# Inputs laid out before the launch: x and memory with features on partitions, weights as one stream of chunks, bias by query and key

## The chip, the cores and the metric

The kernel runs on one core of a Trainium2 chip. A time is the device time of one execution in microseconds (us). What the launching function `kernel()` does with the arrays on the host before the launch is not part of it.

The engines are called as the profile calls them: PE (TensorE, matmuls and transposes), DVE (VectorE), ACT (ScalarE), POOL (GpSimd) and SP (SyncE, which issues most DMAs).

## The reference

One layer of a hybrid decoder trunk, cut to what matters. `x` is 256 tokens of 1024 features, `mem` 256 tokens of 1024; everything is float32.

```
h    = rms_norm(x, mix_norm_g)
qa, ka, va, qb, kb, vb = split(h @ w_in)          # 3072 columns
oa   = rms_norm(attention(qa, ka, va, bias), moba_out_g)   # 8 heads of 64, causal
ob   = rms_norm(diff_attention(qb, kb, vb, bias, lam), subln_g) * (1 - 0.2)  # 4 heads, two softmaxes each
x   += concat(oa, ob) @ w_out
m    = rms_norm(mem, mem_norm_g)
x   += softmax(q(rms_norm(x, cross_norm_g)) k(m)^T / 16) v(m) @ w_co         # w_cq, w_ck, w_cv; 4 heads of 256
h3   = rms_norm(x, ffn_norm_g)
x   += (silu(h3 @ w_gate) * (h3 @ w_up)) @ w_down          # width 2816
out  = rms_norm(x, final_norm_g)
bias[h, t, s] = rel_bias_table[bucket(t - s), h] for s <= t, else -1e30
```

With 256 tokens there is one block of the block-sparse attention, so its selection falls away. `rms_norm(x, g)` is `x * rsqrt(mean(x^2) + 1e-6) * g`.

## The kernel before

All weights pass through one loop of chunks of 1 MB each (128 partitions x 2048 numbers), 65 of them, in the order of their use. SP issues the DMA of a chunk into a raw buffer `wr` (three of them). Then each chunk is split into two float32r halves, a high part `wh` and a low part `wl`, in four quarters (`wpart`, L118): ACT copies `wr` to `wh` (L131), DVE subtracts `wh` from `wr` into `wl` (L116). The activations are split in the same way, and a product is the sum of three matmuls: high by high, high by low, low by high (`ws`, L319, line L325 of the profile). One step of `ws` does this for 128 features and two column halves: six matmuls of 256 columns. A chunk is eight steps.

The order of all work is written by hand. Each engine works its own list in order. `run` (L170) emits a chunk's steps one after the other; after each step `tick` (L148) raises a counter, the slot, and emits whatever was registered for that slot with `at(slot, ...)` or `later(n, ...)`. `tick` also emits quarters of `wpart`, about one for every two slots; `wuse` (L160) emits the quarters of the chunk about to be used that are still missing. So an entry `at(61, mem_t, 0)` puts the first transposes of the memory behind the 61st step on PE, and their evacuations at that place in the lists of ACT and DVE.

The start (L670 to L712). Six matmuls on zeros (`NWARM`) run while the first DMAs are on their way. `x` arrives with tokens on partitions; PE transposes it in 16 pieces (`x_t`, L359) into PSUM, ACT and DVE multiply by the gain and bring it to SBUF (`x_gain`, L367), and `x_split` makes the high and low part. The first chunk of `w_in` is not split: `wf` (L383) multiplies it in plain float32, two matmuls for each of eight feature blocks k, so that PE can start before a split exists. `x_keep` (L379) copies the transposed `x` from PSUM to `xT` for the residual. `x_stats` sums the squares of `x` on ACT; POOL takes the power -1/2; `x_row` (slot 13) spreads it over the partitions with two transposes on PE and a copy `RX` on ACT. `RX` scales the outputs of the projections.

After the first chunk: its product becomes qa0, evacuated by `qk_evac` (DVE), then split by `q_high` (four ACT instructions `qs`, L431) and `q_low` (two DVE, L437), one slot after the other. The second chunk gives ka0 (`qk_evac`, `k_high` on ACT L443, `k_low` on DVE L448), the third qa1, the fourth ka1, then V, then the same for qb and kb.

The bias: a strip of 384 distances for each head is built on POOL from the transposed table (`strips`, L229), written to DRAM and read back with overlapping rows by 12 DMAs (`bias_load`, L258). The gains arrive as rows and are transposed on PE (`load_g`).

The memory: it arrives with tokens on partitions. `mem_stats` (slots 52 and 54) sums squares on ACT, `mem_scale` (58 and 59) scales it on DVE, and `mem_t` (61, 64, 67 and 70) transposes four feature blocks each on PE and splits them on ACT (L310) and DVE (L312). Logits of the second head group follow from slot 73 on (`logits`, matmuls L483 and L484, DVE L489). From `mix_t` on the two kernels have the same list on every engine.

Of the kernel before, what the change touches and what calls it, by code (L numbers as in the profile page):

```python
# [17 lines left out]
P = 128  # L18
# [6 lines left out]
NWARM = 6  # L25
# [10 lines left out]

@with_exitstack
def layer(ctx: ExitStack, tc: tile.TileContext, x, mem, mix_norm_g, w_in, moba_out_g, diff_lambda,
          diff_subln_g, w_out, rel_bias_table, cross_norm_g, mem_norm_g, w_cq, w_ck, w_cv, w_co,
          ffn_norm_g, w_gate, w_up, w_down, final_norm_g, out):  # L40
# [30 lines left out]
    chunks = []  # L71

    def cols(w, c):
        return w[0, :, c * 256:(c + 1) * 256].rearrange("(k p) c -> p k c", p=P), (KT, 256)

    def rows(w, r, c, nk, nc_):
        return (w[0, r * P:(r + nk) * P, c * nc_:(c + 1) * nc_].rearrange("(k p) c -> p k c", p=P),
                (nk, nc_))

    for base in (0, 6):  # L80
        qk = [cols(w_in, base + i) for i in range(4)]
        chunks += [qk[0], qk[2], qk[1], qk[3]]
# [108 lines left out]
    raws[0] = w0  # L191
    state["dma"] = 1
    wdma(2)
    wdma(2)
    memn = slot(3, FT)
# [18 lines left out]

    strip = mx.tile([96, 384], FT, name="strip")
    bias = {}
    nc.gpsimd.memset(strip, NEG)
    tT = const.tile([96, 32], FT, name="tT")
    gvB = const.tile([29, P], FT, name="gvB")
    lp = const.tile([P, 4, 64], FT, name="lp")  # L220
    QL = slot(6).rearrange("p a b -> p (a b)").rearrange("p (n c h s) -> p n c h s", n=2, c=2, h=2)
    nr = 32
    strip_d = dram.tile([nr, 12, 384], FT, name="strip_d")
    sd = strip_d[:, :, :]
# [23 lines left out]
    def small_loads():  # L248
        r = 0
        for gv in (cross_norm_g, mem_norm_g, ffn_norm_g, moba_out_g, diff_subln_g):  # L250
            n = gv.shape[1] // P
            nc.gpsimd.dma_start(gvB[r:r + n, :], gv[0].rearrange("(k p) -> k p", p=P))
            r += n
        nc.gpsimd.dma_start(lp.rearrange("p a b -> p (a b)"),
                            bass.AP(tensor=diff_lambda.tensor, offset=diff_lambda.offset,
                                    ap=[[0, P], [1, 256]]))

    def bias_load(h0, n):  # L258
        t = mx.tile([P, n, 256], FT, name="bias", tag="bias", bufs=2)
# [39 lines left out]

    def transposed(src, j, bank):  # L300

        for a in range(2):
            for t in range(2):
                nc.tensor.transpose(bank[:, a, t * P:(t + 1) * P],
                                    src[:, t, (2 * j + a) * P:(2 * j + a + 1) * P], ident)
# [48 lines left out]
    xT = const.tile([P, KT, S], FT, name="xT")  # L354
    h = hH, hL = hl(both(12))
    hF = slot(4, FT)
    xb = []

    def x_t(k):  # L359

        if k % 4 < 2:
            xb.append(att("xb") if k < 5 else obank("xb").rearrange("p (a b) -> p a b", a=2))
        for t in range(2):
            nc.tensor.transpose(xb[k // 4 * 2 + k % 2][:, k % 4 // 2, t * P:(t + 1) * P],
                                xv[:, t, k * P:(k + 1) * P], ident)

    def x_gain(k):  # L367

        b = xb[k // 4 * 2 + k % 2][:, k % 4 // 2, :]
        if k % 2:  # L370
            nc.vector.tensor_scalar(hF[:, k, :], b, g(G_MIX + k), None, op0=OP.mult)
        else:
            nc.scalar.activation(hF[:, k, :], b, AF.Copy, scale=g(G_MIX + k))
# [5 lines left out]
    def x_keep(j):  # L379
        k = j // 2 * 4 + j % 2  # L380
        nc.vector.tensor_copy(xT[:, k:k + 3:2, :], xb[j])
# [7 lines left out]
    RX = {}  # L389

    def x_stats():
        ss = const.tile([P, 2], FT, name="ssx")
        for t in range(2):
            nc.scalar.activation(sq, xv[:, t, :], AF.Square, accum_out=ss[:, t:t + 1])
        RX[1] = rstd(ss, 2, D, "rx")

# [6 lines left out]
    def load_lambda():  # L403
        ls = const.tile([P, 4], FT, name="ls")
# [9 lines left out]
    KS = slot(0).rearrange("p a b -> p (a b)").rearrange("p (n c h s) -> p n c h s", n=2, c=2, h=2)  # L414
# [199 lines left out]

    def mem_scale(t):
        nc.vector.tensor_scalar(memv[:, t, :], memv[:, t, :], M["r"][:, t:t + 1], None, op0=OP.mult)

    m = (slot(4), slot(5))

    def mem_t(j):  # L620
        bank = att()
        transposed(memv, j, bank)
        split_g(*m, j, bank, G_MEM)
# [14 lines left out]
    for t in range(2):  # L638
        at(52 + 2 * t, mem_stats, t)
    at(56, mem_rstd)  # L640
    for t in range(2):
        at(58 + t, mem_scale, t)
# [9 lines left out]
    for j in range(4):  # L652
        at((61, 64, 67, 70)[j], mem_t, j)
# [16 lines left out]
    load_g(gvA, 0, 8)  # L670
# [10 lines left out]
    for k in (0, 1):  # L681
        x_t(k)
        x_gain(k)
# [9 lines left out]
    for j in range(2):  # L693
        x_keep(j)
# [360 lines left out]
```

## Time and profile before

| | |
|---|---|
| median of 3 runs | 426.32 us (426.26 to 426.61) |
| profiled execution | 426.91 us, of which its span (first to last instruction) is 425.1 us |
| PE busy | 414.4 us, 97% of the span, 2699 matmuls |
| DVE, ACT, POOL busy | 292.7, 253.5 and 27.5 us (69, 60 and 6%) |
| mean granted clock of PE | 0.996 |
| DMA | 74.59 MB, mean 175 GB/s |

The profile is of one execution. Its span leaves 1.8 us of its time outside. "Busy" adds up instructions, and matmuls overlap one another, so a busy PE is not one at its peak; what matters for the end is where PE stands still and how much it has in its list. A releaser ("<-DVE wl L116") is the instruction that ended an idle time, by the profile.

### The profile page before, as it was taken

The numbers are of one execution on the slowest core, as the hardware profiler recorded it, in microseconds if no ns is written. First come the engines' busy times: TensorE is split into PE (matmuls) and PEld (weight loads), VectorE is DVE, ScalarE is ACT, GpSimd is POOL, SyncE is SP. The second block draws the span as 40 slices with busy tenths as digits, with TensorE's granted clock in tenths as the row PEclk, the third lists the DMA queues.
The fourth block names the chain that finished last, engine by engine and source line by source line (L and its number), as shares of the span: only waits on it lengthen the run. The fifth ranks groups of instructions, "written<-read, shape, count | busy, mean of one in ns | idle before, by whom it ended". The sixth has DMA issues, their size and how long they took to land.

```text
span 425.1 us, 7023 instructions
## 1 busy us (share of the span) xinstructions
PE 414.4 (97%) x2699; PEld 375.4 (88%) x2699; DVE 292.7 (69%) x599; ACT 253.5 (60%) x542; POOL 27.5 (6%) x75
## 2 busy tenths in 40 slices
PE   8989999999999999999999999999999999999994
PEld 5888899979998889998889999999888888888883
DVE  3778747899486787586669878888766766544423
ACT  3769978789564664475546665555666566444312
POOL 3840200000010000000000100000000000000001
PEclk9999999999999999999999999999999999999998
DMA  8999743346438525244533765547754575555002
GB/s 254 318 240 311 226 159 100 100 141 202 153 125 293 177 99 200 101 158 139 187 110 100 233 212 191 180 130 235 259 195 131 177 288 198 199 197 197 2 0 99
DMA packets 58257, 74.59 MB, mean 175 GB/s; under 512 B 1708, under 2 KB 50128, under 8 KB 58224
## 3 DMA queue, kind: packets, MB, share of 16 engines
q1 hardware_dynamic: 56528, 69.87, 49.7%
q0 software_dynamic: 1344, 3.88, 3.6%
q8 instruction: 21, 0.34, 0.3%
q10 hardware_dynamic: 352, 0.40, 0.3%
q14 instruction: 12, 0.10, 0.1%
HBM read 72.50 MB, written 1.64 MB: 174 GB/s over the span
## 4 chain that ended last, share of the span: by engine, by line
PE 86%; DVE 5%; ACT 4%; issue 3%; DMA 1%; POOLq 0%; POOL 0%; SPq 0%; DVEq 0%; ACTq 0%
PE acc L325 23%; PE y L347 13%; PE acc L347 9%; PE acc L333 9%; PE att L333 9%; PE att L325 5%; PE att L334 5%; PE acc L334 5%; DVE wl L116 1%; PE att L832 1%; PE oc L876 1%; DMA wr<-in_w_in_dram 1%; ACT qs L431 1%; PE att L506 1%; PE acc L386 1%
## 5 line engine op out<-in xcount | busy, mean ns | idle before, releaser
L116 DVE TENSOR_TENSOR wl<-wr,wh 128x512 fp32r<-128x512 f32 x256 | 163.3, 684 | 35.1 <-ACT wh L131 34.9
L131 ACT ACTIVATE wh<-wr 128x512 fp32r<-128x512 f32 x256 | 144.8, 621 | 51.1 <-issue 22.6
L325 PE MATMUL acc<-b,wh 128*128 128x256 f32 x544 | 101.7, 287 | 0.0
L325 PEld LDWEIGHTS acc<-b,wh 128*128 128x128 f32 x544 | 84.5, 191 | 0.2
L325 PE MATMUL acc<-b,wl 128*128 128x256 f32 x272 | 77.1, 283 | 1.3 <-DVE wl L116 1.3
L325 PEld LDWEIGHTS acc<-b,wl 128*128 128x128 f32 x272 | 52.0, 191 | 1.7 <-DVE wl L116 1.7
L347 PE MATMUL y<-wh,b 128*128 128x512 f32 x152 | 49.0, 391 | 0.0
L347 PE MATMUL acc<-wh,b 128*128 128x512 f32 x128 | 40.5, 397 | 0.0
L333 PE MATMUL acc<-hs,wh 128*128 128x512 f32 x96 | 37.8, 393 | 0.0
L333 PE MATMUL att<-hs,wh 128*128 128x512 f32 x96 | 37.8, 393 | 0.0
L347 PE MATMUL y<-wl,b 128*128 128x512 f32 x88 | 34.2, 389 | 0.0
L347 PEld LDWEIGHTS y<-wh,b 128*128 128x128 f32 x152 | 28.5, 188 | 5.9
L334 PE MATMUL acc<-hs,wl 128*128 128x256 f32 x96 | 27.1, 283 | 0.0
L334 PE MATMUL att<-hs,wl 128*128 128x256 f32 x96 | 27.1, 283 | 0.0
L347 PEld LDWEIGHTS acc<-wh,b 128*128 128x128 f32 x128 | 22.6, 188 | 3.6
L347 PE MATMUL acc<-wl,b 128*128 128x512 f32 x64 | 25.1, 392 | 0.0
L325 PE MATMUL acc<-cHL,wh 128*128 128x256 f32 x128 | 23.4, 283 | 0.0
L325 PE MATMUL att<-b,wh 128*128 128x256 f32 x128 | 23.2, 283 | 0.0
L333 PEld LDWEIGHTS att<-hs,wh 128*128 128x128 f32 x96 | 18.0, 188 | 4.2
L333 PEld LDWEIGHTS acc<-hs,wh 128*128 128x128 f32 x96 | 18.0, 188 | 4.1
L325 PEld LDWEIGHTS att<-b,wh 128*128 128x128 f32 x128 | 20.0, 192 | 0.0
L347 PEld LDWEIGHTS y<-wl,b 128*128 128x128 f32 x88 | 16.6, 189 | 3.6
(225 smaller groups left out, 722.7 us busy)
## 6 DMA issues: line engine op xcount, KB each, us to landing
wr<-in_w_gate_dram SPq DMA_DIRECT2D x11, 1024.0 KB, 5.2
wr<-in_w_up_dram SPq DMA_DIRECT2D x11, 1024.0 KB, 5.3
wr<-in_w_down_dram SPq DMA_DIRECT2D x11, 1024.0 KB, 4.8
wr<-in_w_in_dram SPq DMA_DIRECT2D x9, 1024.0 KB, 5.8
wr<-in_w_ck_dram SPq DMA_DIRECT2D x4, 1024.0 KB, 4.7
wr<-in_w_cv_dram SPq DMA_DIRECT2D x4, 1024.0 KB, 4.9
wr<-in_w_out_dram SPq DMA_DIRECT2D x4, 1024.0 KB, 4.9
wr<-in_w_cq_dram SPq DMA_DIRECT2D x4, 1024.0 KB, 4.7
```

The costliest lines, as they stand in the source:

```text
L116: eng.tensor_tensor(l, t, h, op=OP.subtract)
L131: nc.scalar.activation(h, t, AF.Copy)
L325: nc.tensor.matmul(o[:, c, :], m[:, k, cs], b[:, k, :], start=first and c == 0 and q == 0, stop=last and q == 2, skip_group_check=True)
L333: nc.tensor.matmul(o[c], h[:, k, cs], flat(a[:, k]), start=first, stop=last, skip_group_check=True)
L334: nc.tensor.matmul(o[c][:, 0:256], l[:, k, cs], a[:, k, 0, :], start=False, stop=last, skip_group_check=True)
L347: nc.tensor.matmul(o, m[:, ka, ts], b[:, kw, cs], start=start and q == 0, stop=stop and q == 2, skip_group_check=True)
L386: nc.tensor.matmul(o[:, c, :], w[:, k, c * P:(c + 1) * P], hF[:, k, :], start=k == 0 and c == 0, stop=k == KT - 1, skip_group_check=True)
L431: nc.scalar.activation(qs[to, :, r, :], d[half(r)], AF.Copy)
L506: nc.tensor.transpose(b[:, q * P:(q + 1) * P], e[:, q * P:(q + 1) * P], ident)
L832: nc.tensor.matmul(b[:, t, :], a[:, kt, t * P:(t + 1) * P], k[:, kt, :], start=n == 0, stop=n == 5)
L876: nc.tensor.matmul(o[:, dv, :], v[:, mt, cs], p_[:, mt, :], start=n == 0, stop=n == 5)
```

## The change

The kernel takes other arrays. `kernel()` makes them on the host: `xT` and `memT` with features on partitions, `stream` with every chunk as one block of 128 rows of 8 KB, `gains` with the 37 columns of all norm gains, and `bias` for 128 queries, 12 heads and 256 keys. The transposes, the strip and the gain rows go. The sums of squares now run over partitions: ACT squares two feature blocks at a time, POOL adds the four results into one (three adds), and PE multiplies the sum with ones (`sum_rstd`). The memory is scaled on POOL by a spread row `RM`. Slots are moved.

```diff
-NWARM = 6
+NWARM = 7
...
+    chunks = [(stream[i].rearrange("p (a b) -> p a b", a=a), (a, b)) for i, (a, b) in enumerate(SHAPES)]
...
-    for xlo, xn_, k, nk in ((0, 256, 0, 2), (256, 256, 2, 2), (512, 512, 4, 2), (0, 0, 6, 2)):
-        if xn_:
-            nc.sync.dma_start(xv[:, :, xlo:xlo + xn_], xsrc[:, :, xlo:xlo + xn_])
-        nc.sync.dma_start(w0[:, k:k + nk], src[:, k:k + nk])
+    gT = const.tile([P, 37], FT, name="gT")
+    nc.scalar.dma_start(gT, gains)
...
+    for lo, hi in ((0, 1), (1, 2), (2, 4), (4, 6), (6, 8)):
+        nc.sync.dma_start(xT[:, lo:hi], xt_d[:, lo:hi])
+        (nc.sync if lo else nc.scalar).dma_start(w0[:, lo:hi], src[:, lo:hi])
     state["dma"] = 1
+    wdma(4)
     wdma(2)
-    wdma(2)
...
+        nc.gpsimd.dma_start(t, bias_d[:, h0:h0 + n, :])
...
+    def squares(sqt, src, j):
+
+        ks = slice(2 * j, 2 * j + 2)
+        nc.scalar.activation(sqt[:, ks, :], src[:, ks, :], AF.Square)
+        if j:
+            nc.gpsimd.tensor_tensor(sqt[:, 0:2, :], sqt[:, 0:2, :], sqt[:, ks, :], op=OP.add)
+
+    def sum_rstd(sqt, name):
+
+        b = att()
+        for t in range(2):
+            for a in range(2):
+                nc.tensor.matmul(b[:, 0, 2 * t:2 * t + 2], sqt[:, a, t * P:(t + 1) * P], ones[:, 0:2],
+                                 start=a == 0, stop=a == 1)
+        c = small.tile([P, 2], FT, name="tr", tag="tr", bufs=2)
+        nc.vector.tensor_copy(c, b[:, 0, 0:4:2])
+        return rstd(c, 2, D, name)
...
+    def mem_scale(j):
+        t = memv[:, 2 * j:2 * j + 2, :]
+        nc.gpsimd.tensor_tensor(t, t, M["R"].to_broadcast([P, 2, 256]), op=OP.mult)
...
+    def mem_split(j):
+        if not m:
+            m.extend((slot(4), slot(5)))
+        split_g(*m, j, memv[:, 2 * j:2 * j + 2, :], G_MEM)
...
-    at(13, x_row)
-    at(46, load_g_rest)
-    at(47, load_lambda)
-    at(9, bias_load, 0, 4)
-    at(10, small_loads)
+    at(12, x_rstd)
+    at(14, x_row)
+    at(46, load_lambda)
+    at(10, bias_load, 0, 4)
+    at(18, lambda_dma)
...
-    for t in range(2):
-        at(52 + 2 * t, mem_stats, t)
-    at(56, mem_rstd)
-    for t in range(2):
-        at(58 + t, mem_scale, t)
+    for j in range(4):
+        at(52 + j, mem_squares, j)
+    at(59, mem_rstd)
+    at(62, mem_row)
+    for j in range(4):
+        at(63, mem_scale, j)
+        at((66, 68, 70, 72)[j], mem_split, j)
...
-    for j in range(4):
-        at((61, 64, 67, 70)[j], mem_t, j)
...
+    for j in range(4):
+        for k in (2 * j, 2 * j + 1):
+            x_gain(k)
+            wf(o, w0, k)
+        x_split(j)
+        squares(sqt, xT, j)
     raws.pop(0)
     wdma()
-    wpart()
-    wflush()
-    x_stats()
+    o1 = acc()
+    w1 = raws[1]
+    ready[1] = tuple(wpool.tile([P, KT, 256], FR, name=n, tag=n) for n in ("wh", "wl"))
+    state["part"], state["credit"] = NP + 1, -0.5
+    later(7, qk_evac, o, "qa0", True)
+    run([(wf, (o1, w1, k)) for k in range(2)], done=False)
     for q in range(NP - 1):
         wpart()
         wflush()
-    state["credit"] = 0.5
-    for j in (2, 3):
-        at(8 + 3 * j, x_keep, j)
-    later(6, qk_evac, o, "qa0", True)
-    qk_chunk("ka0", False)
+    run(ws_steps(o1, ready[1], h, range(2, KT)))
+    later(1, qk_evac, o1, "ka0", False)
```

Three places of the lists. First PE at the start, from behind the six matmuls on zeros; `xb` are the transposes of x, `tp` and `gp` those of the table and the gains, `acc<-b,wr` the plain float32 matmuls. Before:

```order
L276 MATMUL gp<-ident,gvA 128x8
L677 LDWEIGHTS still
L677 MATMUL clock<-still 128x512
L364 MATMUL xb<-ident,b_78 128x128 x4
L677 LDWEIGHTS still
L677 MATMUL clock<-still 128x512
L386 MATMUL acc<-b_129,wr 128x256 x2
L234 MATMUL tp<-ident,tr_158 96x32
L364 MATMUL xb<-ident,b_78 128x128 x4
L386 MATMUL acc<-b_129,wr 128x256 x6
L364 MATMUL xb<-ident,b_78 128x128 x8
L386 MATMUL acc<-b_129,wr 128x256 x8
```

Now, from the seventh matmul on zeros:

```order
L202 LDWEIGHTS still
L202 MATMUL clock<-still 128x512
L342 MATMUL acc<-b_125,wr 128x256 x20
L276 MATMUL acc<-b_124,wh 128x256 x2
L276 MATMUL acc<-b_124,wl 128x256
...
L333 MATMUL att<-ones,b_126 128x2 x4
L276 MATMUL acc<-b_124,wh 128x256 x2
```

The plain float32 matmuls stand in one block of 20, of which the last four belong to the second chunk (k = 0 and 1), and the four matmuls with ones stand behind that chunk's steps k = 2 and 3.

Second DVE between the evacuation of qa0 and the low parts of the fourth chunk (chunk 3, counted from 0). Before:

```order
L420 SCALAR_TENSOR_TENSOR qa_326<-acc,RX 128x512
L116 TENSOR_TENSOR wl<-wr,wh 128x512
L437 TENSOR_TENSOR b_123<-qa_326,qs 64x2x256 x2
L116 TENSOR_TENSOR wl<-wr,wh 128x512
L381 COPY xT<-xb 128x2x256
L423 TENSOR_TENSOR ka_360<-acc,RX 128x512
L448 TENSOR_TENSOR b_132<-ka_360,b_132 64x2x256 x2
L116 TENSOR_TENSOR wl<-wr,wh 128x512 x4
```

Now:

```order
L336 COPY tr<-att 128x2
L244 TENSOR_SCALAR rxv<-tr 128x2
L120 TENSOR_TENSOR wl<-wr,wh 128x512
L372 SCALAR_TENSOR_TENSOR qa_252<-acc,RX 128x512
L120 TENSOR_TENSOR wl<-wr,wh 128x512 x3
L389 TENSOR_TENSOR b_122<-qa_252,qs 64x2x256 x2
L375 TENSOR_TENSOR ka_281<-acc,RX 128x512
L400 TENSOR_TENSOR b_129<-ka_281,b_129 64x2x256 x2
L120 TENSOR_TENSOR wl<-wr,wh 128x512 x4
```

The last of the three low parts behind qa0 belongs to chunk 2; ACT has its high part behind the four `qs`. It now stands ahead of both `q_low`, where before one low part stood behind them, and the copy to `xT` is gone.

Third DVE in the memory stage, up to the first logits of the second head group (the `ISA` row); `att,gT` are the memory's low parts read from PSUM, `b_136,gT` the same read from SBUF. Before:

```order
L312 SCALAR_TENSOR_TENSOR b_141<-att,gT,b_140 128x256 x2
L116 TENSOR_TENSOR wl<-wr,wh 128x512 x2
L312 SCALAR_TENSOR_TENSOR b_141<-att,gT,b_140 128x256 x2
L423 TENSOR_TENSOR kb_921<-acc,RX 128x512
L116 TENSOR_TENSOR wl<-wr,wh 128x512 x2
L312 SCALAR_TENSOR_TENSOR b_141<-att,gT,b_140 128x256 x2
L448 TENSOR_TENSOR b_132<-kb_921,b_132 64x2x256 x2
L116 TENSOR_TENSOR wl<-wr,wh 128x512
L312 SCALAR_TENSOR_TENSOR b_141<-att,gT,b_140 128x256 x2
L116 TENSOR_TENSOR wl<-wr,wh 128x512 x2
L489 ISA e,nm<-att,bias 128x128
```

Now:

```order
L375 TENSOR_TENSOR kb_835<-acc,RX 128x512
L120 TENSOR_TENSOR wl<-wr,wh 128x512
L263 SCALAR_TENSOR_TENSOR b_846<-b_136,gT,b_845 128x256 x2
L120 TENSOR_TENSOR wl<-wr,wh 128x512
L400 TENSOR_TENSOR b_129<-kb_835,b_129 64x2x256 x2
L263 SCALAR_TENSOR_TENSOR b_846<-b_136,gT,b_845 128x256 x2
L120 TENSOR_TENSOR wl<-wr,wh 128x512
L263 SCALAR_TENSOR_TENSOR b_846<-b_136,gT,b_845 128x256 x2
L120 TENSOR_TENSOR wl<-wr,wh 128x512
L263 SCALAR_TENSOR_TENSOR b_846<-b_136,gT,b_845 128x256 x2
L120 TENSOR_TENSOR wl<-wr,wh 128x512
L441 ISA e,nm<-att,bias 128x128
```

The evacuation of kb0 moved ahead of all four memory splits; all four now stand between it and the first logits of the second group.

## Rows read from the trace of the kernel before

**Rows 1.** Stretches: length, then busy us (count) of PE, PEld, DVE, ACT, POOL; clock, DMA.
```profile
0.00:6.35 6.35, 4.49 (x14) 1.95 (x14) 0.98 (x4) 2.20 (x4) 1.50 (x10) 1.00 0.66 178
6.35:15.47 9.12, 8.77 (x46) 7.22 (x46) 5.84 (x11) 5.36 (x11) 7.07 (x36) 1.00 1.04 361
15.47:29.32 13.85, 12.56 (x102) 12.13 (x100) 10.44 (x18) 10.86 (x20) 9.20 (x18) 1.00 0.94 238
29.32:91.58 62.26, 61.26 (x450) 57.15 (x451) 46.98 (x127) 50.83 (x125) 3.59 (x6) 1.00 0.59 184
91.58:418.90 327.32, 327.28 (x2091) 296.98 (x2091) 226.96 (x437) 182.93 (x383) 5.61 (x6) 1.00 0.50 168
```

**Rows 2.** PE's instructions in order of time: start, us, what; idle before and releaser.
```profile
1.22 2.74 PE L204 MATMUL clock<-still 128*128 128x512 bf16 x6 [1.22 <-DVE still L201]
...
17.08 0.40 PE L325 MATMUL acc<-b,wh 128*128 128x256 f32 x2
...
29.32 0.39 PE L325 MATMUL acc<-b,wl 128*128 128x256 f32 x1 [1.12 <-DVE wl L116]
...
65.60 0.60 PE L304 MATMUL att<-ident,b 128*128 128x128 f32 x4
65.95 0.48 PE L325 MATMUL acc<-b,wh 128*128 128x256 f32 x2
...
91.58 0.33 PE L483 MATMUL att<-b,qs 128*128 128x128 f32 x1 [0.99 <-DVE b L448]
...
165.94 0.50 PE L799 MATMUL att<-ones,sqa 128*128 128x2 f32 x4
166.31 0.49 PE L325 MATMUL acc<-cHL,wh 128*128 128x256 f32 x2
```

**Rows 3.** The chain that ended last: start, us, engine, tile and line.
```profile
8.20 2.59 PE acc L386 x12
...
20.54 0.67 DVE qa L420
...
115.24 8.64 PE acc L325 x72
```

**Rows 4.** DMAs issued at 1.2 to 1.5 us: KB each, us from issue to landing.
```profile
tb<-in_rel_bias_table_dram ACTq DMA_DIRECT2D x1, 1.5 KB, 4.3
```

**Rows 5.** DMAs issued at 2.2 to 2.5 us.
```profile
wr<-in_w_in_dram SPq DMA_DIRECT2D x1, 256.0 KB, 5.3
```

**Rows 6.** DMAs issued at 3.2 to 3.5 us.
```profile
wr<-in_w_in_dram SPq DMA_DIRECT2D x1, 256.0 KB, 6.3
```

**Rows 7.** DMA issues of the whole execution: KB each, median us to landing.
```profile
wr<-in_w_down_dram SPq DMA_DIRECT2D x11, 1024.0 KB, 4.8
...
wr<-in_w_ck_dram SPq DMA_DIRECT2D x4, 1024.0 KB, 4.7
```

**Rows 8.** DVE's instructions in order of time, as rows 2.
```profile
25.11 0.68 DVE L381 COPY xT<-xb 128x512 f32<-128x512 f32 x1
...
70.68 0.87 DVE L312 SCALAR_TENSOR_TENSOR b<-att,gT,b 128x256 fp32r<-128x256 f32 x2 [1.17 <-ACT b L310]
71.47 0.68 DVE L423 TENSOR_TENSOR kb<-acc,RX 128x512 f32<-128x512 f32 x1
...
74.89 0.87 DVE L312 SCALAR_TENSOR_TENSOR b<-att,gT,b 128x256 fp32r<-128x256 f32 x2 [1.54 <-ACT b L310]
...
79.83 0.28 DVE L489 CUSTOM_DVE_ANT_0 e<-att,bias 128x128 f32<-128x128 f32 x1
```

**Rows 9.** Groups by line and shape: busy us, mean ns of one; idle before.
```profile
L246 POOL MEMSET b<- 64x512 f32 x4 | 2.1, 519 | 0.2
...
L288 POOL TENSOR_TENSOR rb<-rbv,mhalf 128x8 f32<-128x8 f32 x1 | 2.0, 2016 | 14.0 <-DVE rbv L286 14.0
...
L288 POOL TENSOR_TENSOR r<-r2v,mhalf 128x2 f32<-128x2 f32 x1 | 1.1, 1072 | 72.7 <-DVE r2v L286 72.7
...
L288 POOL TENSOR_TENSOR r<-r1v,mhalf 128x2 f32<-128x2 f32 x1 | 0.7, 697 | 45.7 <-DVE r1v L286 45.7
```

More of the change, by code (lines that the diff above doesn't have):

```diff
@@ L34, in rel_buckets, with order, cols, layer @@
     return np.where(n < 16, n, np.minimum(large, 31))
+def order():
+    def cols(w, c):
+        return w, 0, KT, c, 256
+    ids = []
+    for base in (0, 6):
+        ids += [cols("w_in", base + i) for i in (0, 2, 1, 3)]
+        ids += [("w_in", r, 4, 2 if base == 0 else 5, 512) for r in (0, 4)]
+    ids += [cols("w_ck", i) for i in range(4)]
+    ids += [("w_cv", r, 4, 0, 512) for r in (0, 4)]
+    for w in ("w_out", "w_cq"):
+        ids += [cols(w, i) for i in range(4)]
+    ids += [("w_cv", r, 4, 1, 512) for r in (0, 4)]
+    ids += [cols("w_co", i) for i in range(4)]
+    for j in range(NFF // 2):
+        ids += [cols("w_gate", j), cols("w_up", j)]
+    ids += [("w_down", 2 * j, 2, 0, 1024) for j in range(NFF // 2)]
+    return ids
+ORDER = order()
+SHAPES = [(nk, n) for _, _, nk, _, n in ORDER]
 @with_exitstack
-def layer(ctx: ExitStack, tc: tile.TileContext, x, mem, mix_norm_g, w_in, moba_out_g, diff_lambda,
-          diff_subln_g, w_out, rel_bias_table, cross_norm_g, mem_norm_g, w_cq, w_ck, w_cv, w_co,
-          ffn_norm_g, w_gate, w_up, w_down, final_norm_g, out):
+def layer(ctx: ExitStack, tc: tile.TileContext, xt_d, stream, memT, gains, bias_d, diff_lambda, final_norm_g,
+          out):
     nc = tc.nc
@@ L387, in wf, with x_rstd @@
                              stop=k == KT - 1, skip_group_check=True)
[L389 to L395, printed above, removed]
+    def x_rstd():
+        RX[1] = sum_rstd(sqt, "rx")
     def x_row():
@@ L667, in layer @@
         at((108, 112, 124, 127)[j], mix_t, j)
-    load_g(gvA, 0, 8)
     o = acc()
-    w0 = raws[0]
-    state["part"], state["use"], state["done"], state["slot"] = NP, 1, 1, 8
-    def busy(n):
-        for _ in range(n):
-            nc.tensor.matmul(clock, still[:, 0:P], still, start=True, stop=True)
-    busy(1)
-    for k in (0, 1):
-        x_t(k)
-        x_gain(k)
-    busy(1)
-    wf(o, w0, 0)
-    strips()
-    x_split(0)
-    for k in (2, 3):
-        x_t(k)
-        x_gain(k)
-    wf(o, w0, 1)
-    x_split(1)
-    for j in range(2):
-        x_keep(j)
-    for k in (2, 3):
-        wf(o, w0, k)
-    for k in range(4, KT):
-        x_t(k)
-        x_gain(k)
-    x_split(2)
-    x_split(3)
-    for k in range(4, KT):
-        wf(o, w0, k)
+    zeros()
+    state["use"], state["done"], state["slot"] = 2, 1, 8
+    for j in range(4):
[4 more added lines that the diff above has]
+        squares(sqt, xT, j)
     raws.pop(0)
     wdma()
-    wpart()
-    wflush()
-    x_stats()
+    o1 = acc()
[4 more added lines that the diff above has]
+    run([(wf, (o1, w1, k)) for k in range(2)], done=False)
     for q in range(NP - 1):
@@ L1025, in layer, with lay_out, by_k @@
             fin(t, i)
[L1028 to L1030 removed]
 _OUTS = [((1, 256, 1024), 'float32')]
+def lay_out(x, mem, mix_norm_g, w_in, moba_out_g, diff_lambda, diff_subln_g, w_out, rel_bias_table,
+            cross_norm_g, mem_norm_g, w_cq, w_ck, w_cv, w_co, ffn_norm_g, w_gate, w_up, w_down, final_norm_g):
+    def by_k(w):
+        return w.reshape(-1, P, w.shape[1]).transpose(1, 0, 2)
+    stream = np.empty((len(ORDER), P, 2048), np.float32)
+    weights = dict(w_in=w_in, w_out=w_out, w_cq=w_cq, w_ck=w_ck, w_cv=w_cv, w_co=w_co, w_gate=w_gate, w_up=w_up,
+                   w_down=w_down)
+    for i, ((name, r, nk, c, n), shape) in enumerate(zip(ORDER, SHAPES)):
+        w = weights[name][0][r * P:(r + nk) * P, c * n:(c + 1) * n]
+        stream[i] = by_k(w).reshape(P, 2048)
+    norms = np.concatenate([v[0] for v in (mix_norm_g, cross_norm_g, mem_norm_g, ffn_norm_g, moba_out_g,
+                                           diff_subln_g)])
+    away = 128 + np.arange(P)[:, None] - np.arange(S)[None, :]
+    bias = rel_bias_table[rel_buckets()[np.maximum(away, 0)]].transpose(0, 2, 1)
+    bias = np.where(away[:, None, :] >= 0, bias, np.float32(NEG))
+    return {"xT": by_k(x[0].T), "stream": stream, "memT": by_k(mem[0].T), "gains": norms.reshape(-1, P).T,
+            "bias": bias, "diff_lambda": diff_lambda, "final_norm_g": final_norm_g}
 def kernel(**inputs):
```

131 lines of the change are left out of this document (23 added, 108 removed).

## The prediction

> **What bounds the kernel now.** I first read the page's engine table: PE is busy 97% of the span, so only a shorter list on PE or an idle time of PE that goes away can help. The stretches come next [rows 1]: each gives its length and PE's busy time, and the difference is what PE stands still. That is 1.86 us before 6.35 (6.35 − 4.49), 0.35 up to 15.47, 1.29 up to 29.32, 1.00 up to 91.58, and 0.04 in the remaining 327.32 us. The reader should see that the last 77% of the kernel has no idle time to give, and that its list is the same in both kernels: whatever the change does is decided before 91.58. PE's list in time [rows 2] puts names to the gaps: 1.12 us at 29.32 ended by a `wl` of DVE, and 0.99 us at 91.58 ended by the low part of a key. The chain [rows 3] shows the same path at the start: plain float32 matmuls on PE, the evacuation of qa0 on DVE at 20.54, then PE alone. DVE, the DMA queues and POOL follow, as sources of prices.
>
> **The stream of weights in 8 KB rows.** `w_ck`, whose rows are 1 KB, lands a chunk in 4.7 us and `w_down`, with rows of 4 KB, in 4.8 [rows 7]. So longer rows are worth nothing in the steady state, where in addition PE has no idle time that a DMA ends. I cost this at 0; hidden behind PE, it can give neither gain nor loss while three buffers run ahead.
>
> **The start.** 16 transposes of `x` go from PE and 20 plain matmuls stand in one block. In the chain 12 records of such matmuls take 2.59 us [rows 3], 0.216 each; a matmul is two records, so a feature block (two matmuls) costs 0.864 us and the twenty 8.64. When can they start? The ACT queue's first DMA, issued at 1.2 to 1.5, lands 4.3 us later [rows 4], so about 5.7 for the first weights and gains, which now use that queue. A quarter of a chunk issued at 2.2 takes 5.3 [rows 5] and lands at 7.5; with `x_gain` behind it I let the blocks k = 2 and 3 begin at 7.8. A piece issued at 3.2 takes 6.3 [rows 6], 9.5 at the latest for the fourth piece and some 10.4 for the fifth, while PE needs it for k = 6 at 7.8 + 4 × 0.864 = 11.3: not binding. Eight blocks from 7.8 on (k = 2 to 7 and the two of the second chunk) end at 14.7, where step k = 2 of the second chunk begins. Before, this same step began at 17.08 [rows 2], behind two split steps of its chunk. PE is 2.4 us earlier here; the bounds are 1.2 (last pieces late, 15.9) and 4.0 (no landing binds, start at 6.2 and 13.1).
>
> Then come additions. Two matmuls with 2 columns against ones take 0.37 us (165.94 to 166.31, four records [rows 2]), the four of `sum_rstd` 0.74. A step of `ws` is six matmuls, and 72 matmuls take 8.64 us [rows 3]: 0.72. The evacuation of qa0 waits for `RX`, so for slot 14: 14.7 + 2 × 0.72 + 0.74 + 2 × 0.72 = 18.3, and an estimated 0.8 us for spread, copy and arrival, 19.1, against 20.54 before: 1.5 earlier. Between slots 12 and 14 POOL must take a power. Before, one such instruction took 0.70 to 2.02 us [rows 9]; with 2 × 0.72 + 0.74 = 2.2 us of PE's work between them it fits, at 2.02 barely.
>
> From qa0 to the `wl` that PE waits for at 29.32 it was 8.78 us on DVE and ACT. The new order has one low part of chunk 2, which waits for its high part behind the four `qs` on ACT, ahead of both `q_low`, where before it stood behind. So the two `q_low`, 0.68 each by the neighbouring 64x512 rows, come behind that wait: +1.36; the copy to `xT`, 0.68 [rows 8], goes. 8.78 + 0.68 = 9.5, and 19.1 + 9.5 = 28.6: PE resumes 0.7 us earlier than at 29.32. PE arrives 2.4 − 0.74 = 1.7 us earlier and so waits 1.1 + 1.7 − 0.7 = 2.1 there. That is the choice on which the forecast rests: the start's gain is given back at this wait. From both sides: −2.2 (ACT gets to the high part at once, 1.5 earlier and the copy saved) and +0.6 (a two-fold delay of the `qs`).
>
> **The memory stage.** PE loses 16 transposes: four take 0.35 us (65.60 to 65.95 [rows 2]), sixteen 1.40. It gains four matmuls with ones (0.74) and two spreads (0.18, half of four transposes), net −0.48. The stall of 0.99 at 91.58: DVE waited 1.17 and 1.54 us for ACT, which waited for these transposes [rows 8], and kb0 was evacuated at 71.47 behind the first of them. The new list has kb0 ahead: 71.47 − 1.17 − 0.87 = 69.4. Behind it up to the logits stand one evacuation, five `wl` and two `k_low` at 0.68 and four pairs of splits at 0.87: 8 × 0.68 + 3.48 = 8.9, so 78.3 against 79.83: 1.5 earlier, if none of these waits. With PE 0.48 earlier at the stall, 0.99 + 0.48 = 1.47 is the most; I take 0.8 of the 0.99, for one short wait left over: −1.3. If the splits wait as before, it is −0.48.
>
> **POOL's new work.** Three adds each for x and memory and four scalings are elementwise on 128x512 with two inputs. The trace has no such instruction. From below: a MEMSET of 512 columns, 0.52; from above: the power on 128x8, 2.02; I take 1.05, at the r2 power's 1.07 [rows 9]. Four scalings from slot 63 (about 68 us) end at 72.2, or 76.1 at the upper price, and the splits want them at slots 66 to 72, 71.6 to 76.6: hidden by either. [...]
>
> **The sum.** −0.7 − 1.3 + 0 = −2.0. The profiled execution took 426.91 us (span 425.1 and 1.8 around it); 2.0 less is 424.9. The median of the runs is 426.32, 0.6 below the profiled one, so 424.3. Its own range: 423.0 to 425.5.
>
> **The rivals.** *A: the wait at 29.32 doesn't bind.* If ACT reaches the high part early, PE keeps its head start: −2.4 + 0.74 − 1.12 − 0.2 for the rest of the 1.29 us idle in that stretch, and −1.47 in the memory stage: −4.4, 421.9. For it: DVE is busy 10.44 of the 13.85 us there [rows 1], so it is not the instructions' own time that fills the 8.78. Against: the stall there is already 1.12, and DVE's list up to it gets longer by 0.68.
>
> *B: POOL holds up DVE.* On the other side. DVE's `wl` (two inputs in SBUF) and POOL's scalings could exclude one another; the place is the memory stage, where up to 91.58 DVE has 1.5 us in hand. The r2 power, while `wl` ran, took 1.07, the r1 power 0.70 [rows 9], same shape: a sign of it, though the times on POOL are rough. Price: four scalings of 1.05 delay DVE by 4.2 if each blocks in full; of that 2.0 only uses up the gain. So it is slower from 2.0 us of delay on, 426.3 + 2.2 = 428.5 in full and 426.4 at half. The point is whether DVE's `wl` beside a scaling lasts longer than 0.69. [...]
>
> [...]
>
> *The change does not do what it says* holds partly: sums over partitions put 0.74 us twice on PE, so its list shortens by 0.48 in the memory stage only.
>
> **How the numbers follow.** Forecast 0.62, A 0.17, B 0.15 (half of it slower, half same; its middle is 426.4), C 0.06. Two runs of this kernel are told apart from 0.2% on: same is 425.47 to 427.17. The forecast's case falls in same for about a tenth of its weight (stage 2 at −0.48 and the wait in full). Faster: 0.62 × 0.9 + 0.17 = 0.73, and a little of B at a quarter price, 0.75. Same 0.13, slower 0.12. The range goes below to A with 0.3 for its landings (421.6) and above to half of B (426.6); beyond lie the full price of B and part of C, 0.15.
>
> **What would show it.** In the profile after: step k = 2 of the second chunk at 14.7 (13.1 says no landing binds, 15.9 that a late one does); PE's stall before a step of chunk 3 grown to about 2.1 and ended by `wl` (A: under 0.8); the idle time before the second group's logits under 0.3; the last stretch again 327.3 long. [...] The prediction fails if the stall in chunk 3 is neither grown nor ended by `wl`, or if PE has a new stall behind 91.58.

## The result, and the profile after

The changed kernel takes 430.16 us (median; 430.01 to 430.64) against 426.29 (426.13 to 426.61): slower, ratio 1.0092 (95% interval 1.0074 to 1.0109). The forecast was 424.3, with 421.6 to 426.6 as its range.

Of the 3.87 us between the medians, the two profiled executions show 2.7 in the span (425.1 and 427.8). The rest lies elsewhere: the profiled execution of before was 0.6 above its median, that of the changed kernel 0.15 below, and 2.2 us of the changed kernel's time lie outside its span against 1.8. Why that last 0.4 differs no run here settles. The variants below show 2.1 to 2.2 while POOL keeps all its places (the e_ runs) and 1.7 to 1.8 where its sums or scalings went to DVE (the c_ runs and d_best2), in every execution.

The stretches of the changed kernel, cut at the places that answer to the cuts of before [rows 1, 2]: the second chunk's step k = 2, the first low part that PE waits for, the second group's logits. Columns: window, length, then busy us and count of PE, PEld, DVE, ACT, POOL, granted clock, DMA share, GB/s.

```profile
0.00:15.14 15.14, 12.92 (x47) 8.59 (x48) 7.29 (x11) 9.33 (x17) 6.69 (x15) 1.00 0.86 274
15.14:30.23 15.09, 12.23 (x98) 11.59 (x96) 9.46 (x17) 8.65 (x16) 3.48 (x6) 0.99 0.95 353
30.23:94.51 64.28, 61.99 (x443) 57.87 (x443) 48.80 (x125) 51.22 (x126) 11.49 (x9) 0.98 0.40 142
94.51:421.80 327.29, 327.24 (x2091) 296.97 (x2091) 226.95 (x437) 182.94 (x383) 5.64 (x6) 1.00 0.47 168
```

The last stretch is as long as before (327.29 and 327.32), as forecast. The first ends 1.94 us earlier than before's step at 17.08. All of that is lost by 30.23, where before stood at 29.32, and the third stretch is 2.02 us longer than the 62.26 of before, though PE's list in it is shorter. Behind the cut at 15.14 something else is new: a clock under 1.00. PE's list of the changed kernel, the instructions at these places:

```profile
4.88 2.50 PE L342 MATMUL acc<-b,wr 128*128 128x256 f32 x8 [0.50 <-DMA wr<-in_stream_dram]
7.85 7.64 PE L342 MATMUL acc<-b,wr 128*128 128x256 f32 x32 [0.47 <-DMA wr<-in_stream_dram]
...
17.15 0.95 PE L333 MATMUL att<-ones,b 128*128 128x2 f32 x8
17.96 0.48 PE L276 MATMUL acc<-b,wh 128*128 128x256 f32 x2
...
30.23 0.58 PE L276 MATMUL acc<-b,wl 128*128 128x256 f32 x1 [2.63 <-DVE wl L120]
...
89.92 0.83 PE L458 MATMUL att<-ident,e 128*128 128x128 f32 x3 [1.19 <-DVE e L480]
94.51 0.33 PE L435 MATMUL att<-b,qs 128*128 128x128 f32 x1 [1.03 <-DVE b L400]
```

The stall before the fourth chunk grew from 1.12 to 2.63 us, and one stall of 0.99 in the memory stage became two, 2.2 together. Cut finer, the third stretch begins like this (same columns as above):

```profile
29.00:30.00 1.00, 0.00 (x0) 0.00 (x0) 0.97 (x2) 1.00 (x3) 0.00 (x0) 0.93 0.82 336
30.00:31.00 1.00, 0.77 (x3) 0.77 (x4) 1.00 (x3) 0.88 (x2) 0.00 (x0) 0.50 0.39 164
31.00:32.00 1.00, 1.00 (x7) 1.00 (x6) 1.00 (x3) 0.00 (x0) 0.00 (x0) 0.50 0.06 25
32.00:33.00 1.00, 1.00 (x7) 1.00 (x7) 0.58 (x1) 0.38 (x1) 0.00 (x0) 0.50 0.08 8
33.00:34.00 1.00, 1.00 (x9) 1.00 (x9) 0.68 (x1) 0.96 (x3) 0.00 (x0) 0.86 0.55 156
```

Behind 2.63 us without a matmul the granted clock is 0.50 until about 33.2. Three matmuls take 0.64 us there (31.26 to 31.90) and 0.36 where it is 1.00 again (33.58 to 33.94). So, as an estimate from these two, the 3.0 us at 0.50 hold about 1.3 us that no wait in any list shows.

DVE's list says where the stall comes from, and why the memory stage is late (start, us, instruction; idle before and releaser):

```profile
8.41 1.36 DVE L313 TENSOR_SCALAR b<-xT,gT 128x256 f32<-128x256 f32 x1
...
14.38 2.62 DVE L120 TENSOR_TENSOR wl<-wr,wh 128x512 fp32r<-128x512 f32 x3 [0.35 <-ACT wh L135]
...
20.63 0.69 DVE L372 SCALAR_TENSOR_TENSOR qa<-acc,RX 128x512 f32<-128x512 f32 x1 [1.52 <-ACT RX L255]
21.23 1.29 DVE L120 TENSOR_TENSOR wl<-wr,wh 128x512 fp32r<-128x512 f32 x2
24.58 0.69 DVE L120 TENSOR_TENSOR wl<-wr,wh 128x512 fp32r<-128x512 f32 x1 [2.06 <-ACT wh L135]
25.19 1.38 DVE L389 TENSOR_TENSOR b<-qa,qs 64x512 fp32r<-64x512 f32 x2
26.61 0.69 DVE L375 TENSOR_TENSOR ka<-acc,RX 128x512 f32<-128x512 f32 x1
28.05 1.40 DVE L400 TENSOR_TENSOR b<-ka,b 64x512 fp32r<-64x512 f32 x2 [0.76 <-ACT b L395]
29.49 2.50 DVE L120 TENSOR_TENSOR wl<-wr,wh 128x512 fp32r<-128x512 f32 x4
...
72.61 1.01 DVE L120 TENSOR_TENSOR wl<-wr,wh 128x512 fp32r<-128x512 f32 x1
73.54 2.95 DVE L263 SCALAR_TENSOR_TENSOR b<-b,gT,b 128x256 fp32r<-128x256 f32 x2
...
82.75 0.28 DVE L441 CUSTOM_DVE_ANT_0 e<-att,bias 128x128 f32<-128x128 f32 x1
```

And POOL's list, the instructions that lie beside them:

```profile
8.36 1.26 POOL L326 TENSOR_TENSOR b<-b 128x512 f32<-128x512 f32 x1 [4.59 <-ACT b L324]
...
13.96 1.28 POOL L326 TENSOR_TENSOR b<-b 128x512 f32<-128x512 f32 x1 [1.53 <-ACT b L324]
...
70.53 5.68 POOL L572 TENSOR_TENSOR b<-b,RM 128x512 f32<-128x512 f32 x4 [1.90 <-ACT RM L255]
```

Beside POOL's first sum (8.36 to 9.62) a gain takes 1.36 us on DVE, where the two before it took 0.35; beside the second (from 11.16) the next takes 1.44. Beside the third (13.96 to 15.24) the first three low parts take 2.62, where three elsewhere take 1.90. Beside the scalings (70.53 to 76.21) a pair of splits takes 2.95, where before it took 0.87 [rows 8]. The logits come at 82.75, before at 79.83.

At the start PE feels it. PEld is the loading of a matmul's weights on PE; two of its rows show what it waited for:

```profile
12.63 2.46 PEld L342 LDWEIGHTS acc<-b,wr 128*128 128x128 f32 x12 [0.43 <-DVE b L313]
...
15.85 0.19 PEld L276 LDWEIGHTS acc<-b,wl 128*128 128x128 f32 x1 [0.33 <-DVE wl L120]
```

The first waits for the gain of 1.44 us, the second for the first of those three low parts, which alone took 1.42.

### The profile page after: what moved, and what is told of

The parts are those of the page before. It is cut to its first block, busy times and chain, and to the rows that moved or that the text cites. A ratio compares the mean times of both kernels' runs of the same rounds, so it can differ in the third digit from the quotient of the medians.

```text
span 427.8 us, 6928 instructions
## 1 busy us (share of the span) xinstructions
PE 414.5 (97%) x2677; PEld 375.0 (88%) x2677; DVE 294.0 (69%) x591; ACT 253.4 (59%) x542; POOL 27.9 (7%) x36
## 3 DMA queue, kind: packets, MB, share of 16 engines
HBM read 72.50 MB, written 1.05 MB: 172 GB/s over the span
## 4 chain that ended last, share of the span: by engine, by line
PE 86%; DVE 7%; ACT 3%; issue 2%; DMA 1%; POOL 0%; SPq 0%; POOLq 0%; DVEq 0%; ACTq 0%
PE acc L276 24%; PE y L298 13%; PE acc L298 9%; PE acc L284 9%; PE att L284 9%; PE att L276 5%; PE att L285 4%; PE acc L285 4%; DVE wl L120 2%; PE att L765 1%; PE oc L809 1%; DVE b L263 1%; ACT qs L383 1%; DMA xT<-in_xT_dram 1%; PE att L458 1%
## 5 line engine op out<-in xcount | busy, mean ns | idle before, releaser
L450 ACT ACTIVATE e<-e,nm 128x128 f32<-128x128 f32 (+1 forms) x32 | 14.3, 447 | 9.5 <-DVE nm L441 9.5
```

The lines of the kernel that those rows point to most:

```text
L450: nc.scalar.activation(e[:, cs], e[:, cs], AF.Exp, bias=nm[:, t:t + 1], scale=-1.0, accum_out=lsum[:, i, t:t + 1])
```

## The experiments

Three theories came out of this. The stall at 30.23 is made by the order of the lists behind qa0; it costs a second time through the clock; and POOL's reading instructions hold DVE up. The rivals: qa0 alone is late, the slow matmuls come from something beside them, POOL is only late itself.

**e_fill.** Ten matmuls on zeros fill the stall.

```diff
     qk_chunk("qa1", True)
+    for _ in range(10):
+        nc.tensor.matmul(clock, still[:, 0:P], still, start=True, stop=True)
     qk_chunk("ka1", False)
```

Expected: 

> Ten matmuls of 512 columns on zeros stand in PE's list between the third and the fourth chunk, where PE stood still for 2.63 us before the low part released it at 30.23, and the granted clock was 0.50 from 30.2 to 33.2 us. Theory (the long stall costs a second time, through the clock): the release stays at 30.2, the granted clock stays at 1.00 behind it, and the 3.0 us at half speed become 1.5: about 1.5 us shorter than the changed kernel's 430.16, 428.7. Rival (the slow matmuls there come from something else, such as transfers or DVE beside them): the clock stays at 0.50 and the time at 430.2, or it grows by what the ten matmuls overrun.

Measured: 428.68 us (428.61 to 428.94), 1.48 less than the changed kernel. PE's list in e_fill, from the filler on, and the second group's logits:

```profile
27.20 2.33 PE L652 MATMUL clock<-still 128*128 128x512 bf16 x10
29.18 0.59 PE L276 MATMUL acc<-b,wh 128*128 128x256 f32 x2
30.24 0.38 PE L276 MATMUL acc<-b,wl 128*128 128x256 f32 x1 [0.47 <-DVE wl L120]
...
93.19 0.33 PE L435 MATMUL att<-b,qs 128*128 128x128 f32 x1 [1.02 <-DVE b L400]
```

The microsecond behind the release in e_fill, columns as in the stretches:

```profile
31.00:32.00 1.00, 1.00 (x10) 1.00 (x10) 1.00 (x3) 0.00 (x0) 0.00 (x0) 1.00 0.18 74
```

The low part releases PE at 30.24 as it did at 30.23, and the two stalls of the memory stage are as they were (1.20 and 1.02); only the clock stays up (1.00 from 31 to 32, where it was 0.50). The logits come 1.3 us earlier (93.19 against 94.51). More work on PE made the kernel faster: the second price of the stall is shown, 1.3 us in the profiled pair and 1.48 between the medians.

**e_cred15.** The splitting of weights starts two quarters earlier.

```diff
-    state["part"], state["credit"] = NP + 1, -0.5
+    state["part"], state["credit"] = NP + 1, 1.5
```

Expected: 

> Only the starting credit of the weight splitting is changed, from -0.5 to 1.5: two quarters of splitting move ahead, two of the third chunk ahead of RX on ACT, and the first of the fourth chunk ahead of the four copies of qa0, its low part ahead of the low part of ka0 on DVE. Theory (the order on DVE and ACT behind qa0 sets the stall at 30.23): the stall of 2.63 us shrinks to 1.1 or less and stands one quarter later, the clock stays at 1.00, and the kernel is 1.5 + 1.5 = 3.0 us shorter than 430.16: 427.2. Rival (the late qa0 at 20.63 alone sets it, whatever stands where): the stall stays over 2 us and the time within 0.5 us of 430.2.

Measured: 426.99 us (426.77 to 427.36), 3.17 less. The stall is not shorter but gone, so the theory was even too cautious; qa0 is as late as ever. DVE's list in e_cred15:

```profile
20.77 0.69 DVE L372 SCALAR_TENSOR_TENSOR qa<-acc,RX 128x512 f32<-128x512 f32 x1 [1.52 <-ACT RX L255]
...
25.34 0.68 DVE L120 TENSOR_TENSOR wl<-wr,wh 128x512 fp32r<-128x512 f32 x1
26.18 1.39 DVE L400 TENSOR_TENSOR b<-ka,b 64x512 fp32r<-64x512 f32 x2 [0.16 <-ACT b L395]
27.58 1.90 DVE L120 TENSOR_TENSOR wl<-wr,wh 128x512 fp32r<-128x512 f32 x3
```

The stretch of the former stall in e_cred15:

```profile
20.00:30.00 10.00, 10.00 (x85) 10.00 (x86) 7.75 (x13) 7.52 (x13) 1.45 (x3) 1.00 1.01 378
```

The first low part of the fourth chunk stands ahead of the key's low part now (25.34), and PE is busy 10.00 of 10.00 us. It was the order of the lists. Later stalls remain: one of 1.60 us before the second group's logits (in the changed kernel two, 2.2 together), and a new one of 0.99 at 237 us.

**e_x11.** The sum with ones one slot earlier, `at(11, x_rstd)`.

Expected: 

> Only the sum of the squares of x with ones moves from slot 12 to slot 11, ahead by one step of PE (0.72 us). Theory (RX and so qa0 were late because the way from the sum over the power to the spread row takes 2.6 us, and they set the stall at 30.23): qa0 is evacuated at about 19.9 instead of 20.63, PE resumes at 29.5, the kernel is 0.7 us shorter than 430.16, and 2.1 shorter in the executions where the clock then stays up behind the shorter stall of 1.9 us. Rival (qa0 waits for its own slot, not for RX): qa0 stays at 20.6 and the time at 430.2.

Measured: 429.78 us (429.62 to 430.06), 0.38 less, not 0.7. The sum went from 17.15 to 16.46, but the row stands at slot 14, which PE reaches at 19.51; in the changed kernel it had waited there only until 19.74. So qa0 came at 20.34, 0.29 earlier, and PE resumed at 29.95, 0.28 earlier; the stall (2.62) stayed over 2 us, and the granted clock fell behind it as well (0.50 from 32.5 to 33.5). The wait for POOL's power was a small part of qa0's lateness, 0.23 us; the forecast of this run was nearly twice too high, and its rival (qa0 stays at 20.6) did not hold either.

**e_memset.** POOL is as busy but reads nothing: the scaling is left out, and the memory is a constant.

```diff
-        nc.gpsimd.tensor_tensor(t, t, M["R"].to_broadcast([P, 2, 256]), op=OP.mult)
+        for _ in range(3):
+            nc.gpsimd.memset(t, 0.5)
```

Expected: 

> The four scalings of the memory on POOL (two inputs read from SBUF, 1.42 us each) are replaced by three fills of the same tile, which read nothing; the memory is left unscaled and replaced by a constant. Theory (reading POOL instructions and DVE ones exclude one another): DVE's pair of memory splits at 73.5 falls from 2.95 us to 0.87 and the low part of the weights before it from 1.01 to 0.69, though POOL is as busy; the two stalls at 89.9 and 94.5 (2.2 us together) shrink to 1.0 or less: 1.2 us or more shorter than 430.16, 429.0. Rival (POOL is only late, it doesn't hold DVE up): the DVE instructions fall to their old lengths only as they get their data, and the time changes by less than 0.5 us.

Measured: 427.75 us (426.19 to 428.98; executions with a mean clock of 0.990 to 0.997), 2.4 less at the medians. PE's list in e_memset at the two places, then DVE's:

```profile
30.38 0.38 PE L276 MATMUL acc<-b,wl 128*128 128x256 f32 x1 [2.64 <-DVE wl L120]
...
92.42 0.33 PE L435 MATMUL att<-b,qs 128*128 128x128 f32 x1 [0.29 <-DVE b L400]
...
72.92 0.68 DVE L120 TENSOR_TENSOR wl<-wr,wh 128x512 fp32r<-128x512 f32 x1
73.52 0.88 DVE L263 SCALAR_TENSOR_TENSOR b<-b,gT,b 128x256 fp32r<-128x256 f32 x2
```

POOL's list in e_memset, what lies beside it:

```profile
68.91 6.59 POOL L573 MEMSET b<- 128x512 f32 x12
```

At the same moment, with POOL at work until 75.5, the pair takes 0.88 instead of 2.95. The stall of 1.19 is gone and the last one is 0.3, and the stretch from the release to the logits is 62.04 us instead of 64.28. That POOL's scalings, which read SBUF, hold DVE up, and that neither a busy POOL nor late data does, is shown. The gains at the start have one tensor input and a factor for each partition; beside POOL's sums they are slowed as well, from 0.35 to 1.36 and 1.44.

**c_dveadd.** With the credit of 1.5, the three sums of x go to DVE (`eng = nc.vector if src is xT else nc.gpsimd`).

Expected: 

> On top of the credit of 1.5 (426.99 us): the three sums of x's squares go from POOL to DVE, 0.6 us each. Theory (POOL's sums hold up DVE's gains at the start, 1.45 us instead of 0.35 twice): both gains take 0.35, the last plain matmul ends some 0.4 us earlier and the kernel is 0.3 to 0.6 us shorter, 426.5. Rival (the start is set by the landing of the pieces): nothing changes, 427.0.

Measured: 426.99 us (426.62 to 427.35), no change against e_cred15. All four gains take 0.35 again, yet the first split matmul starts at 16.02, in e_cred15 at 15.31, and a piece's landing holds PE (0.37 us at 10.95). The rival's number came, but the run changed a second thing. Without the sums POOL reaches its first bias load (512 KB) at 3.71 us, in e_cred15 at 15.34. POOL and PE in c_dveadd:

```profile
3.71 0.70 POOL L233 DMA_DIRECT2D bias<-in_bias_dram  x1
10.95 5.42 PE L343 MATMUL acc<-b,wr 128*128 128x256 f32 x24 [0.37 <-DMA wr<-in_stream_dram]
```

The weight piece issued at 4.2 to 5 us (KB, us to landing), first in c_dveadd, then in e_cred15:

```profile
wr<-in_stream_dram SPq DMA_DIRECT2D x1, 256.0 KB, 6.5
```

```profile
wr<-in_stream_dram SPq DMA_DIRECT2D x1, 256.0 KB, 4.4
```

So the landing that holds PE is 2.1 us slower with the bias load beside it. The two steps up to the sum with ones are faster without POOL's sums (1.62 us, 16.02 to 17.64, against 2.01 in the changed kernel, 15.14 to 17.15), and the profiled span is 0.4 longer (425.2 against 424.8) while less time lies outside it. What POOL's hold costs at the start is not separated by this run and stays open.

**e_rows.** Chunks as blocks of short rows.

```diff
-    chunks = [(stream[i].rearrange("p (a b) -> p a b", a=a), (a, b)) for ...
+    chunks = [(stream[i].rearrange("p n -> (p n)").rearrange("(a p b) -> p a b", a=a, p=P), (a, b)) for ...
...
-        stream[i] = by_k(w).reshape(P, 2048)
+        stream[i] = w.reshape(P, 2048)
```

Expected: 

> The stream is stored so that a chunk lies as blocks of 128 short rows (1 KB for most chunks, 2 or 4 KB for the others) instead of 128 rows of 8 KB; nothing else differs from the changed kernel. Theory (row length is worth nothing, since PE waits for no transfer after the start): within 0.4 us of 430.16, the landing times of full chunks 4.7 to 5.3 us as before. Rival (8 KB rows give something in the start, where 16 DMA engines are full): the pieces of the first chunks land up to 1 us later and the kernel is 0.5 to 1.5 us longer.

Measured: 429.95 us (429.14 to 430.53), the same as the changed kernel within what the runs scatter. Full chunks land in 5.5 us, by the DMA issues of e_rows (KB each, median us to landing):

```profile
wr<-in_stream_dram SPq DMA_DIRECT2D x62, 1024.0 KB, 5.5
```

The same row of the changed kernel, with 8 KB rows:

```profile
wr<-in_stream_dram SPq DMA_DIRECT2D x62, 1024.0 KB, 4.8
```

The executions differ: two of 429.1 with a mean clock of 0.998, three of 430.0 to 430.5 with 0.991 or 0.992, and the profiled one is of the first kind and has the same stall of 2.63 and no fall of the clock. So the clock fell in three of these five executions, by their means, and not in the other two. At equal clock (e_fill, 428.68, against 429.14) the short rows cost about 0.5: the rival's size, found by comparing across kernels and so no more than likely. The trace puts it at the start: PE resumes behind the stall at 30.77, in the changed kernel at 30.23.

**c_early2 and c_best.** With the credit of 1.5 the memory's statistics go to slots 46 to 54 and its scaling to DVE at 55; c_best adds c_dveadd and e_x11.

```diff
-        at(52 + j, mem_squares, j)
-    at(59, mem_rstd)
-    at(62, mem_row)
-        at(63, mem_scale, j)
+        at(46 + j, mem_squares, j)
+    at(51, mem_rstd)
+    at(54, mem_row)
+        at(55, mem_scale, j)
...
-        nc.gpsimd.tensor_tensor(t, t, M["R"]...
+        nc.vector.tensor_tensor(t, t, M["R"]...
```

Expected of c_early2: 

> On top of the credit of 1.5 (426.99 us): the memory's squares and sums move to slots 46 to 54, and the four scalings go from POOL to DVE at slot 55, where DVE stood idle for 2.2 and 3.5 us before 53.5 and 59.1. Theory (with POOL reading beside it, DVE is late by some 2.5 us in the memory stage, and that makes the stall of 1.60 us before the second group's logits): DVE's pair of splits takes 0.87 instead of 2.94, the stall of 1.60 is 0.3 or less: 1.3 to 1.6 us shorter, 425.5. Rival (four more DVE instructions of 0.6 and POOL's three sums, now beside a busier DVE, cost as much): 426.5 to 427.5.

Expected of c_best: 

> The credit of 1.5, the memory's statistics earlier with its scaling on DVE, the sums of x on DVE, and the sum with ones one slot earlier (slot 11). Theory: the gains add up, 426.99 - 1.5 - 0.4 = 425.1, and the earlier sum adds nothing, since behind the new credit PE has no stall near 27 us that qa0 sets; about 1.3 us faster than the kernel before. Rival (DVE has no idle time left between 20 and 92 us, so each of the parts pushes the next): 426 or more.

Measured: 427.63 (427.07 to 428.41) and 427.54 (425.60 to 429.75). Neither forecast held; c_best's time lies where its rival put it and c_early2's just above, but not for the rivals' reasons. The memory stage is as the theory says, PE busy 35.00 of 35.00 us from 60 to 95, but a new wait stands ahead of it. PE's list in c_early2:

```profile
52.63 1.05 PE L333 MATMUL att<-ones,b 128*128 128x2 f32 x8 [1.24 <-POOL b L326]
```

The stretch around it in c_early2:

```profile
30.00:60.00 30.00, 28.76 (x188) 26.33 (x188) 19.39 (x58) 23.14 (x61) 5.43 (x5) 0.94 0.48 173
```

The sum with ones comes before POOL has added, and the granted clock is 0.94 over the 30 us around this wait of 1.24, PE's only one there (busy 28.76). In c_best, which has c_dveadd's early bias load too, the wait is 1.76; the profiled execution shows no fall behind it (1.00 from 30 to 60), and its executions reach from 425.6 at a mean clock of 0.997 to 429.75 at 0.990: for one and the same program.

**d_best2.** The credit of 1.5 stays, the sums of x stay on POOL, the sums of the memory get their time (slots 44 to 47, 53, 57, scaling on DVE at 58), and the credit is given back.

```diff
+    at(150, lambda: state.update(credit=state["credit"] - 2.0))
...
+        at(44 + j, mem_squares, j)
+    at(53, mem_rstd)
+    at(57, mem_row)
+        at(58, mem_scale, j)
```

Expected: 

> The credit of 1.5, given back at slot 150 (it left a new stall of 0.99 us at 237 us); the memory's squares at slots 44 to 47, their sum with ones at 53 instead of 51 (where PE waited 1.2 to 1.8 us for POOL's sums), the row at 57, the scaling on DVE at 58; the sums of x and the slot of their product with ones as in the changed kernel. Theory: no stall over 0.5 us is left on PE between 16 and 418 us, nothing lowers the clock, and the time is 426.99 - 1.6 - 1.0 = 424.4; some 2 us faster than the kernel before. Rival (the scaling at slot 58 meets the first evacuation of qb0 and pushes DVE's list): the stall before the second group's logits stays at 1 us or more, 425.5 or more.

Measured: 422.77 us (422.72 to 422.85): ratio to the kernel before 0.9908 (0.9892 to 0.9925), faster than both, and 1.6 better than expected. Of the 1.6, 0.4 lies outside the span (1.8 here, 2.2 in e_cred15); the rest is not explained. The stretches of d_best2, from the second chunk to the second group's logits:

```profile
15.30:30.00 14.70, 14.39 (x119) 13.95 (x118) 12.20 (x21) 10.76 (x19) 3.37 (x5) 1.00 0.99 375
30.00:60.00 30.00, 30.00 (x214) 27.73 (x214) 20.16 (x60) 24.79 (x64) 5.84 (x5) 1.00 0.54 195
60.00:91.00 31.00, 31.00 (x234) 29.44 (x233) 30.34 (x75) 27.70 (x67) 0.00 (x0) 1.00 0.39 137
```

No stall is left in these from 30 on (the 0.31 before it lie ahead of 20 us), the clock is 1.00 throughout, and the four executions lie within 0.13 us.

## Why the prediction was wrong, point by point

**Right.** The change decides itself before the second group's logits; the stream is worth about nothing; the start's lead is given back at the first low part of the fourth chunk. The way from qa0 to that release was forecast as 9.5 us, and it is 9.6 (20.63 to 30.23).

**Three steps failed**: the start's term was mis-sized, POOL's new work and the clock behind the stall were put at nothing.

**The start, mis-sized by 1.6 us.** qa0 was evacuated at 20.63, not 19.1, and −0.7 became +0.9. Step k = 2 began at 15.14, not 14.7: the third piece released PE at 7.85 (forecast 7.8), but the sixteen plain matmuls took 7.29 us, not 6.91. The two steps up to the sum took 2.01 instead of 1.44, the sum 0.81 instead of 0.74, and from there to qa0 it was 2.67 instead of 2.24, of which 0.23 was the wait for POOL's power. The rows name POOL's sums as a cause of the first two: PEld waited for a gain and a low part that took twice their time or more beside them. How much of the 1.6 that is, no run separates.

**POOL's new work was put at nothing.** The sum took it as hidden, because the scaled memory is ready before the splits want it. It was ready when DVE's splits came; but the four scalings held up DVE's own instructions, and that cost 2.2 us of the memory stage (64.28 against 62.04 in e_memset). Rival B said so, with its sign and the row by which to know it; its chance of 0.15 was too low, and it looked at the memory stage alone, not at the sums of the start. A scaling took 1.42 us, over the 1.05 that I took and within the bounds (0.52 to 2.02). DVE lost 2.1 us on one pair of splits and 0.3 on the low part before it, some 2.4 of the 4.2 that B prices in full.

**The stall was costed at its length.** The sum let PE wait 2.1 us and counted those 2.1; it waited 2.63, and the clock took another 1.3 (1.48 between the medians), as e_fill measures. Rival C, with its chance of 0.06 and its part in the range, was a lower clock at the start, behind the matmuls on zeros. No run shows that term: the granted clock was 1.00 there throughout, and the sixteen plain matmuls took 0.23 us a record (7.29 us, 32 records). The forecast itself lengthened a stall, and that was the place to ask.

**The memory stage.** −1.3 became +2.0. With the clock up it is +0.7 (62.95 us in e_fill, 30.24 to 93.19, against 62.26). Take both away, the clock's 1.3 and POOL's 2.2, and an estimated 60.7 is left, some 1.5 under before, where the sum had 1.3. So what the sum said of transposes, stall and DVE's list there held; the two terms at nothing were what failed.

**Together.** The profiled spans: −1.94 at the start, +2.85 up to the release, +2.02 behind it, −0.23 at the end: 2.7, where −2.0 was forecast. The measured time is 5.9 above the forecast: 4.7 in the span, 0.4 outside it, and 0.8 because the changed kernel's profiled execution does not lie 0.6 above its median as that of before did. B's slower branch gave 428.5, and with the clock on top it comes near 430.16; that is luck, since DVE lost about half of what that branch counts, and the start, which it left at −0.7, made up for the rest.

## What to carry to other kernels

A gap on PE had two prices here, its length (2.63 us) and what the clock took behind it (1.3 us); where a forecast makes a stall longer, ask for the second price at that stall, and try a filler before a new order. POOL and DVE were not free of each other here where both read SBUF (a pair of splits took 2.95 us beside POOL's scalings and 0.88 beside its fills): an instruction moved to an idle POOL was paid on DVE where DVE was full. Work taken off an engine also moves up what stands behind it in that engine's list: in c_dveadd a load started 11.6 us earlier and spoiled the test. When a lead at the start changes nothing, look at which queue the first late operand stands in: here two quarters of credit, one number, were worth 3.2 us.

## What the runs showed of the hardware that was not expected

- Ten more matmuls made the kernel 1.48 us shorter, by keeping the clock up (1.00 in e_fill's microsecond from 31, 0.50 in the changed kernel's).
- The clock's fall behind a stall isn't the same in every execution: with 2.63 us it came in the changed kernel's profiled execution (0.50) and not in that of e_rows (1.00), whose executions took 429.1 or some 430.0 to 430.5 us; in c_early2, with a wait of 1.24 us, the clock was 0.94 over the 30 us around it, and in c_best's profiled execution, with 1.76, it was 1.00.
- A two-input instruction on POOL of 128x512 took 1.26 to 1.28 us by itself in its list and 1.42 on average in the row of four scalings; a gain on DVE went from 0.35 to 1.36 beside it, and a weight's low part from 0.69 to 1.42 at 62.15.
- Chunks in short rows landed 0.7 us later (5.5 against 4.8), and the kernel's time hardly moved.
